# Where a head pair's k and v parts and the gates live: from three SBUF pools to the latents' pool and DRAM

## The chip, the cores and the metric

The kernel runs on one core of one Trainium2 chip. The metric is the time of one execution in device microseconds, from three runs. Engines are named as in the profile: PE is TensorE (PEld its weight loads), DVE VectorE, ACT ScalarE, POOL GpSimd, SP SyncE, which here issues nearly all DMAs.

## The reference

Two layers work on 512 tokens of width 2048. The first is a pooling mixer with a SiLU gate. The second, which this change touches, is latent attention with 16 heads, block-causal in blocks of 128 queries:

```python
c = rmsnorm(c, kv_latent_g)
kv = (c @ kv_w_b).reshape(B, S, N_HEADS, QK_NOPE + V_HEAD)
q = (rmsnorm(q_lat, q_latent_g) @ w_q_b).reshape(B, S, N_HEADS, QK_HEAD)
o = chunk_causal_attention(q, k, v).reshape(B, S, W_B)
return x + (o * jax.nn.silu(gate)) @ w_out
```

The gate is a product of the normalised stream with 2048 columns of `w_in`; each head has 128 of them. k and q get a norm over 192 elements and a rotary part of 64.

## The kernel before

Every float32 matrix product is done as three products of float32r parts: an operand is split into hi (a cast on ACT) and lo (a subtraction on DVE), and hi·hi, hi·lo and lo·hi are added in PSUM. `split` and `load_w` do this, so each weight tile of 128x512 costs a DMA issue on SP, a cast on ACT (L125) and a subtraction on DVE (L126). Raw weight tiles have three buffers, the parts four.

The kernel is written with a tile framework: the program says what is computed, and pools give out buffers under a tag. A scheduler places the instructions on each engine in its own order when the program is built and gives each tile a free buffer of its pool. The pools that matter here are `apool` (32 tiles of 128x512, called the latents' pool here), `bpool` (32), `xpool` (16) and the temporary pool `tpool3` (7).

After the first layer the stream is spilled to DRAM (L485) and two normalised copies stand as parts in `apool` and `bpool`. From them come the k/v latent and the q latent: four pairs of parts each, 16 tiles of `apool`, which every head pair reads. Then come the gates: `gate_unit` (L576 on) multiplies a head's gate columns, scales the result into a temporary tile, and writes the SiLU of it to a tile of `apool`, which is kept to the end. Sixteen gates and the two latents fill `apool`. The parts of the stream for the gates stay in `bpool` until the last gate.

Heads go in eight pairs. The preparation of a pair (`prep_units`) loads the weights, makes four k/v products, one for each block of 128 tokens (`kv_unit`, L612 to L614), and from each a raw k and the parts of v, then k statistics, four q products (L632 to L634) with their rotary part on POOL (L680 to L683), q statistics, and six transposes (`tr_unit`, L708 and L695) whose results are split. Raw k stands in two tiles of `xpool`; v in four tiles of `bpool`, or of `xpool` for the first pair.

The attention of a pair (`attn_units`) has, for each head, four score units (L738; the maximum L741, its scaling L743, Exp L746, all for one block of queries, with up to 512 keys), then four transposes of P (L757), and two P·V units (L782 to L784). The second P·V unit ends with the product of output and gate (L787), in place of the gate.

The order of the program is written at the end of the file. Attention units of pair n and preparation units of pair n+1 are merged by due times: `LEAD` (0.421 of a pair) says how far preparation goes ahead, `PACE` stretches the attention. For the last pair the units merged in are others: `og_unit`, which splits the gated output of a head, and `out_unit`, the output product for three of the 16 column blocks, head by head (L143 to L145 there). Gate units 0 to 11 stand before the preparation of pair 0, gate units 12 to 15 after it. At the end come the other column blocks, each added to the spilled stream (`out_store`).

Of the kernel before, what the change touches and what calls it, by code (L numbers as in the profile page):

```python
# [7 lines left out]
F32 = mybir.dt.float32  # L8
F32R = mybir.dt.float32r
I32 = mybir.dt.int32  # L10
AF = mybir.ActivationFunctionType
# [3 lines left out]
P = 128  # L15
S = 512
# [5 lines left out]
NH = 16  # L22
# [29 lines left out]
def trunk_kernel(  # L52
# [16 lines left out]
    nc = tc.nc  # L69
    V, A, G, T = nc.vector, nc.scalar, nc.gpsimd, nc.tensor  # L70
# [4 lines left out]
    dpool = ctx.enter_context(tc.tile_pool(name="dpool", bufs=16, space=bass.MemoryType.DRAM))  # L75

    def xt(shape=(P, S), dt=F32):
        return xpool.tile(list(shape), dt, tag="x", name="xt")

    def at(dt=F32R):  # L80
        return apool.tile([P, S], dt, tag="a", name="at")

    def bt(shape=(P, S), dt=F32R):
        return bpool.tile(list(shape), dt, tag="b", name="bt")
# [4 lines left out]
    def tt_(n=S, dt=F32):  # L89
        return tp[0].tile([P, n], dt, tag="t", name="tt_")  # L90
# [4 lines left out]
    def sc():  # L95
        return ps.tile([P, S], F32, tag="sc", name="sc", bufs=2)
# [4 lines left out]
    def f(ap):  # L101
        return ap.bitcast(F32)
# [13 lines left out]
    def load_w(src, n, parts=None):  # L116

        raw = wpool.tile([P, S], F32, tag="raw", name="raw")
        if parts is None:
            hi = wpool.tile([P, S], F32R, tag="whi", name="whi", bufs=4)  # L120
            lo = wpool.tile([P, S], F32R, tag="wlo", name="wlo", bufs=4)
        else:
            hi, lo = parts(), parts()
        nc.sync.dma_start(raw[:, :n], src)
        A.copy(hi[:, :n], raw[:, :n])  # L125
        V.tensor_tensor(lo[:, :n], raw[:, :n], f(hi[:, :n]), ALU.subtract)  # L126
        return hi, lo

    def proj(w, nk, xs, m=P, acc=None):

        acc = acc or mm()
        c = S // m if m == P else 4
        for k0 in range(0, nk, c):
            hi, lo = load_w(w[:, k0 * m:(k0 + c) * m], c * m)
            for j in range(c):
                k = k0 + j
                mm3(acc[:m, :], hi[:, j * m:(j + 1) * m], lo[:, j * m:(j + 1) * m], xs[k],
                    k == 0, k == nk - 1)
        return acc
# [7 lines left out]
    def split(src, hi, lo):  # L147
        A.copy(hi, src)
        V.tensor_tensor(lo, src, f(hi), ALU.subtract)
# [112 lines left out]
    with ExitStack() as c1:  # L262
# [91 lines left out]
        with ExitStack() as c2:  # L354
            hp = c2.enter_context(tc.tile_pool(name="hp", bufs=2, **tile_))
            for j in range(NJ):
# [5 lines left out]
                hi = w7.tile([P, 4, 2, P], F32R, tag="hi", name="hi")  # L362
                lo = w7.tile([P, 4, 2, P], F32R, tag="lo", name="lo")
# [8 lines left out]
                a, b = xh[j], xl[j]  # L372
# [46 lines left out]
    apool = ctx.enter_context(tc.tile_pool(name="apool", bufs=32, **tile_))  # L419
# [8 lines left out]
    def pooled_tile(g, o):  # L428
        x = tt_()
        nc.sync.dma_start(x, raws[g * 8 + o])  # L430
        if g:
            x = pool_tile(x, g * 8 + o in neg, WINS[g])
        hi, lo = at(), at()
        split(x, hi, lo)
        return hi, lo
# [15 lines left out]
    for g in range(NG):  # L451
        ys = [y_tile(g, o, pooled) for o in range(8)]
        if g == 0:
            rope_tables()
            for k in range(KD):
                x = xt()
# [14 lines left out]
    for k in range(KD):  # L471
        hi, lo = at(), at()
        gsplit(xr[k], C_GKV + k, hi, lo)
        xkv.append((hi, lo))
        hi, lo = bt(), bt()
        gsplit(xr[k], C_GB + k, hi, lo)
        xb.append((hi, lo))
        if k < 2:
            A.activation(accs[k], xr[k], AF.Square)
        else:  # L480
            sq = tt_()
            A.activation(sq, xr[k], AF.Square)
            V.tensor_tensor(accs[k % 2], accs[k % 2], sq, ALU.add)
        dsp = dpool.tile([P, S], F32, tag="dsp", name="dsp")
        nc.sync.dma_start(dsp, xr[k])  # L485
        spill.append(dsp)
# [10 lines left out]
    def latent_norm(lat, gcol):  # L497
        ac = tt_()
        A.activation(ac, lat[0], AF.Square)
        for o in range(1, 4):  # L500
            sq = tt_()
            A.activation(sq, lat[o], AF.Square)
            V.tensor_tensor(ac, ac, sq, ALU.add)
        r = norm_r(ac, 512)
        res = []
        for o in range(4):
            V.scalar_tensor_tensor(lat[o], lat[o], cs[:, gcol + o:gcol + o + 1], r, ALU.mult, ALU.mult)
            hi, lo = at(), at()
            split(lat[o], hi, lo)
            res.append((hi, lo))  # L510
        return res
# [62 lines left out]
    gates = []  # L574

    def gate_unit(o):  # L576
        acc = proj(bwin[4 + o], KD, xb)
        z = tt_()
        V.tensor_tensor(z, acc, rb[0], ALU.mult)
        sg = at(F32)  # L580
        A.activation(sg, z, AF.Silu)
        gates.append(sg)


    gqk = const.tile([P, 1], F32, name="gqk")
    V.tensor_tensor(gqk, cs[:, C_GKN:C_GKN + 1], cs[:, C_GQN:C_GQN + 1], ALU.mult)
    SC = 192.0 ** -0.5
    st = {}

    def small(n=8, tag="sm", bufs=6):  # L590
        return spool.tile([P, n], F32, tag=tag, name=tag, bufs=bufs)

    def hg_begin(hg):
        d = {}
        d["kvw"] = [load_w(wkvb[hg, :, k * 512:(k + 1) * 512], 512) for k in range(4)]
        d["kraw"] = [xt((P, 2, 256)) for _ in range(2)]
        d["qraw"] = [None] * 4
        vt = bt if hg else xt
        d["vh"] = [vt((P, 2, 256), F32R) for _ in range(2)]
        d["vl"] = [vt((P, 2, 256), F32R) for _ in range(2)]  # L600
        d["ssk"] = small(8, "ssk", 2)
        d["ssq"] = small(8, "ssq", 2)
        st[hg] = d
# [122 lines left out]
    def score_unit(hg, h, i):  # L726
        d = st[hg]
        n = (i + 1) * P
        s = sc()
        kh, kl = d[("T", h)]  # L730
        krh, krl = d["kr"][h]
        qh, ql_ = d[("T", 3 + h)]
        qr = d["qr"][h]
        qs = slice(i * P, (i + 1) * P)
        ops = [(qh[:, qs], kh[:, 0:n]), (qh[:, qs], kl[:, 0:n]), (ql_[:, qs], kh[:, 0:n]),
               (qr[:, qs], krh[:, 0:n]), (qr[:, qs], krl[:, 0:n])]
        for j, (l, r) in enumerate(ops):
            T.matmul(s[:, 0:n], l, r, start=(j == 0), stop=(j == 4))  # L738
        V.memset(s[0:64, n - 64:n], -1e30)
        nm = small(1, "nm", 4)  # L740
        V.tensor_reduce(nm, s[:, 0:n], AX.X, ALU.max)  # L741
        rq = d["rq"][:, 2 * i + h:2 * i + h + 1]
        V.scalar_tensor_tensor(nm, nm, -1.0, rq, ALU.mult, ALU.mult)  # L743
        pe = tt_()
        sm = small(1, "sm", 4)
        A.activation(pe[:, 0:n], s[:, 0:n], AF.Exp, bias=nm, scale=rq, accum_out=sm)  # L746
        V.reciprocal(sm, sm)
        V.tensor_scalar(pe[:, 0:n], pe[:, 0:n], sm, None, ALU.mult)
        d[("P", h, i)] = pe
# [18 lines left out]
    def pv_unit(hg, h, pr):  # L768
        d = st[hg]
        if pr == 0:  # L770
            d["ov"] = ps.tile([P, S], F32, tag="ov", name="ov", bufs=1)
        ov = d["ov"]
        js = range(2 * pr + 2)
        for j in js:
            c0 = P if j == 2 * pr + 1 else 0
            dst = ov[:, pr * 256 + c0:pr * 256 + 256]
            ph = d["pth"][j // 2][:, j % 2, c0:256]
            pl = d["ptl"][j // 2][:, j % 2, c0:256]
            vh = d["vh"][j // 2][:, j % 2, h * P:(h + 1) * P]
            vl = d["vl"][j // 2][:, j % 2, h * P:(h + 1) * P]  # L780
            last = j == js[-1]
            T.matmul(dst, vh, ph, start=(j == 0), stop=False)  # L782
            T.matmul(dst, vh, pl, start=False, stop=False)
            T.matmul(dst, vl, ph, start=False, stop=last)  # L784
        if pr == 1:
            gt = gates[2 * hg + h]
            V.tensor_tensor(gt, ov, gt, ALU.mult)  # L787

    def prep_units(hg):
        def q(t):  # L790
            q_unit(hg, t)
            qrot_unit(hg, t)

        f = {"B": lambda: hg_begin(hg), "K": lambda: kstats_unit(hg), "S": lambda: qstats_unit(hg)}
        for t in range(4):
            f[f"k{t}"] = lambda t=t: kv_unit(hg, t)
            f[f"q{t}"] = lambda t=t: q(t)
        for u in range(6):
            f[f"T{u}"] = lambda u=u: tr_unit(hg, u)
        return [f[o] for o in PREP]  # L800
# [16 lines left out]
    ogs = [None] * NH  # L817

    def og_unit(h):
        nt = at if h < 14 else bt  # L820
        hi, lo = nt(), nt()
        split(gates[h], hi, lo)
        ogs[h] = (hi, lo)

    first3 = {}
# [13 lines left out]
        V.tensor_tensor(x, x, acc, ALU.add)  # L839
        nc.sync.dma_start(outT[o], x)  # L840

    nhg = NH // 2
    for o in range(12):
        gate_unit(o)
    for u in prep_units(0):
        u()
    for o in range(12, NH):
        gate_unit(o)
# [23 lines left out]
    for u in fill[j:]:  # L872
        u()
    og_unit(14)
    og_unit(15)
    for o in range(NO, NO + 2):
        for k0, n in ((0, 4), (4, 4), (8, 4), (12, 2)):
# [69 lines left out]
```

## Time and profile before

| | |
|---|---|
| three runs, median (lowest, highest) | 1953.45 us (1952.83, 1954.7) |
| the profiled execution | 1959.55 us, span 1957.8 us |
| mean granted TensorE clock | 0.997 |
| PE, PEld, DVE, ACT, POOL busy | 1924.6, 1712.1, 1274.9, 819.9, 257.9 us |
| instructions | 30554 |
| DMA, mean | 120 GB/s |

Busy times are sums of instructions on an engine over one profiled execution. Matmuls are pipelined, so PE's busy time says that a matmul was under way, not that PE was at its peak. Stages by time: the spill starts near 1120 us; spill, latents and gates follow until near 1497, attention until 1811, and the output product until the end.

### The profile page before, as it was taken

Reading aid. Unit: us, or ns where it says so; the run is one execution under the profiler, and the core shown is the slowest. Engines: PE = TensorE matmul, PEld = TensorE weight load, DVE = VectorE, ACT = ScalarE, POOL = GpSimd, SP = SyncE. Lnnn points to the kernel's source line nnn. Section 1 sums busy time; section 2 is a strip of 40 time slices with the busy share of each in tenths; the row PEclk is TensorE's granted clock in tenths of the full one; section 3 lists DMA queues with packets and bytes.
Section 4 is the critical chain, followed back from the end, with each engine's and each line's share of the span. In section 5 each row is a group of like instructions: output and inputs, shape, how many; then the busy total and the mean of one; then the engine's idle time right before and its main releaser. Section 6 shows DMA issues by size and latency. Waiting matters only on the chain.

```text
span 1957.8 us, 30554 instructions
## 1 busy us (share of the span) xinstructions
PE 1924.6 (98%) x11356; PEld 1712.1 (87%) x11356; DVE 1274.9 (65%) x2289; ACT 819.9 (42%) x1562; POOL 257.9 (13%) x405
## 2 busy tenths in 40 slices
PE   7999999999999999999999999999999999999999
PEld 6999999999999878888888888888888888888887
DVE  8577786796666677486595567473344788797432
ACT  7343333333333443233333354333254777785221
POOL 0433332333233100000000000000010111110000
PEclk9999999999999999999999999999999999999999
DMA  6454444435443464344344344323322111121632
GB/s 190 149 160 154 150 132 127 130 119 164 134 135 125 151 209 158 109 124 144 119 128 130 111 148 128 92 92 99 97 93 79 53 42 47 50 68 49 219 118 86
DMA packets 167893, 235.52 MB, mean 120 GB/s; under 512 B 14656, under 2 KB 94912, under 8 KB 167744
## 3 DMA queue, kind: packets, MB, share of 16 engines
q1 hardware_dynamic: 166992, 232.84, 37.8%
q8 instruction: 89, 1.46, 0.3%
q10 hardware_dynamic: 720, 0.73, 0.1%
q14 instruction: 60, 0.49, 0.1%
q0 software_dynamic: 32, 0.00, 0.0%
HBM read 208.35 MB, written 25.17 MB: 119 GB/s over the span
## 4 chain that ended last, share of the span: by engine, by line
PE 89%; DVE 4%; DMA 3%; ACT 2%; issue 1%; SPq 0%; DVEq 0%; ACTq 0%
PE mm L145 16%; PE mm L143 16%; PE mm L144 16%; PE k L331 9%; PE k L329 9%; PE k L327 9%; PE sc L738 2%; PE mm L612 2%; DMA raw<-awin 2%; PE mm L614 2%; PE mm L613 2%; DVE lo L311 1%; PE k L378 1%; PE mm L632 1%; PE k L379 1%
## 5 line engine op out<-in xcount | busy, mean ns | idle before, releaser
L125 ACT CAST whi<-raw 128x512 fp32r<-128x512 f32 (+2 forms) x421 | 253.4, 609 | 519.8 <-PE mm L144 448.0
L329 PE MATMUL k<-xl,hi 128*128 128x256 f32 x1680 | 460.7, 283 | 0.0
L327 PE MATMUL k<-xh,hi 128*128 128x256 f32 x1680 | 460.7, 283 | 0.0
L126 DVE TENSOR_TENSOR wlo<-raw,whi 128x512 fp32r<-128x512 f32 (+2 forms) x421 | 281.4, 671 | 235.2 <-ACT whi L125 233.2
L331 PE MATMUL k<-xh,lo 128*128 128x256 f32 x1680 | 418.8, 284 | 2.6 <-DVE lo L311 2.5
L310 ACT CAST hi<-raw 128x1792 fp32r<-128x1792 f32 x120 | 202.8, 1690 | 368.2 <-PE k L331 248.2
L311 DVE TENSOR_TENSOR lo<-raw,hi 128x1792 fp32r<-128x1792 f32 x120 | 248.1, 2068 | 158.3 <-ACT hi L310 158.0
L145 PE MATMUL mm<-bt,wlo 128*128 128x512 f32 x860 | 335.5, 390 | 0.2 <-DVE wlo L126 0.2
L143 PE MATMUL mm<-bt,whi 128*128 128x512 f32 x860 | 334.6, 389 | 0.0
L144 PE MATMUL mm<-bt,whi 128*128 128x512 f32 x860 | 334.5, 389 | 0.0
L327 PEld LDWEIGHTS k<-xh,hi 128*128 128x128 f32 x1680 | 323.3, 192 | 0.0
L329 PEld LDWEIGHTS k<-xl,hi 128*128 128x128 f32 x1680 | 323.2, 192 | 0.0
L331 PEld LDWEIGHTS k<-xh,lo 128*128 128x128 f32 x1680 | 297.5, 192 | 4.2 <-DVE lo L311 3.6
L143 PE MATMUL mm<-at,whi 128*128 128x512 f32 x516 | 201.9, 393 | 4.2 <-ACT whi L125 4.2
L145 PE MATMUL mm<-at,wlo 128*128 128x512 f32 x516 | 202.7, 393 | 0.6 <-DVE wlo L126 0.3
L144 PE MATMUL mm<-at,whi 128*128 128x512 f32 x516 | 202.7, 393 | 0.0
L145 PEld LDWEIGHTS mm<-bt,wlo 128*128 128x128 f32 x860 | 161.4, 188 | 34.5 <-DVE wlo L126 0.6
L143 PEld LDWEIGHTS mm<-bt,whi 128*128 128x128 f32 x860 | 161.5, 188 | 33.8 <-ACT whi L125 0.2
L144 PEld LDWEIGHTS mm<-bt,whi 128*128 128x128 f32 x860 | 161.5, 188 | 33.4
L306 POOL TENSOR_TENSOR raw<-raw 128x256 f32<-128x256 f32 x120 | 99.4, 828 | 440.6 <-DVE raw L304 415.8
L143 PEld LDWEIGHTS mm<-at,whi 128*128 128x128 f32 x516 | 97.4, 189 | 25.1 <-ACT whi L125 5.3
L145 PEld LDWEIGHTS mm<-at,wlo 128*128 128x128 f32 x516 | 97.6, 189 | 22.7 <-DVE wlo L126 2.6
(1151 smaller groups left out, 2584.0 us busy)
## 6 DMA issues: line engine op xcount, KB each, us to landing
raw<-awin SPq DMA_DIRECT2D x240, 256.0 KB, 3.2
raw<-awo SPq DMA_DIRECT2D x128, 256.0 KB, 2.9
raw<-bwin SPq DMA_DIRECT2D x80, 256.0 KB, 2.7
raw<-awg SPq DMA_DIRECT2D x64, 256.0 KB, 2.8
raw<-bwo SPq DMA_DIRECT2D x59, 256.0 KB, 2.8
scr<-e SPq DMA_DIRECT2D x56, 256.0 KB, 2.7
raw<-wkvb SPq DMA_DIRECT2D x32, 256.0 KB, 2.9
raw<-wqb SPq DMA_DIRECT2D x32, 192.0 KB, 2.4
```

The source lines that it names most:

```text
L125: A.copy(hi[:, :n], raw[:, :n])
L126: V.tensor_tensor(lo[:, :n], raw[:, :n], f(hi[:, :n]), ALU.subtract)
L143: T.matmul(dst, wh, xh, start=first, stop=False)
L144: T.matmul(dst, wh, xl, start=False, stop=False)
L145: T.matmul(dst, wl, xh, start=False, stop=last)
L306: G.tensor_tensor(c[:, :, 6, :], c[:, :, 4, :], c[:, :, 2, :], ALU.add)
L310: A.copy(hi, c[:, :, 1:8, :])
L311: V.tensor_tensor(lo, c[:, :, 1:8, :], f(hi), ALU.subtract)
L327: T.matmul(dst, hi[:, j % 2, wi, :], xh[j][:, xi, :], start=first, stop=False, skip_group_check=True)
L329: T.matmul(dst, hi[:, j % 2, wi, :], xl[j][:, xi, :], start=False, stop=False, skip_group_check=True)
L331: T.matmul(dst, lo[:, j % 2, wi, :], xh[j][:, xi, :], start=False, stop=last, skip_group_check=True)
L612: T.matmul(acc, ch[:, tsl], hi, start=(k == 0), stop=False)
```

## The change

k products and v parts of every pair are taken from `apool`, which has 16 buffers for this once the gates are out of it. A gate unit writes SiLU in place in its temporary tile and stores it to DRAM. At the third score unit of a head its gate is loaded to a tile of `apool`. The product with the output is made there; for the first seven pairs the result is stored to DRAM, over the gate, and for the last pair the tile is kept. `og_unit` loads the gated output of heads 0 to 13 into a temporary tile and splits it from there; heads 0 to 7 have their parts in `apool`, the others in `bpool` (before: 0 to 13 and 14 to 15).

```diff
-    def at(dt=F32R):
-        return apool.tile([P, S], dt, tag="a", name="at")
+    def at(dt=F32R, shape=(P, S)):
+        return apool.tile(list(shape), dt, tag="a", name="at")
@@ gate_unit
-        sg = at(F32)
-        A.activation(sg, z, AF.Silu)
-        gates.append(sg)
+        A.activation(z, z, AF.Silu)
+        gd = dpool.tile([P, S], F32, tag="gd", name="gd")
+        nc.sync.dma_start(gd, z)
+        gates.append(gd)
@@
-    st = {}
+    st, gated = {}, {}
+    nhg = NH // 2
@@ hg_begin
-        d["kraw"] = [xt((P, 2, 256)) for _ in range(2)]
+        d["kraw"] = [at(F32, (P, 2, 256)) for _ in range(2)]
         d["qraw"] = [None] * 4
-        vt = bt if hg else xt
-        d["vh"] = [vt((P, 2, 256), F32R) for _ in range(2)]
-        d["vl"] = [vt((P, 2, 256), F32R) for _ in range(2)]
+        d["vh"] = [at(F32R, (P, 2, 256)) for _ in range(2)]
+        d["vl"] = [at(F32R, (P, 2, 256)) for _ in range(2)]
@@ score_unit
+        if i == 2:
+            gt = d[("G", h)] = at(F32)
+            nc.sync.dma_start(gt, gates[2 * hg + h])
@@ pv_unit
         if pr == 1:
-            gt = gates[2 * hg + h]
+            gt = d.pop(("G", h))
             V.tensor_tensor(gt, ov, gt, ALU.mult)
+            if hg == nhg - 1:
+                gated[2 * hg + h] = gt
+            else:
+                nc.sync.dma_start(gates[2 * hg + h], gt)
@@ og_unit
-        nt = at if h < 14 else bt
+        nt = at if h < 8 else bt
         hi, lo = nt(), nt()
-        split(gates[h], hi, lo)
+        if h < 14:
+            x = tt_()
+            nc.sync.dma_start(x, gates[h])
+        else:
+            x = gated[h]
+        split(x, hi, lo)
```

## Rows read from the trace of the kernel before

**Rows 1.** Page, busy time of each engine, its share and instructions.
```profile
PE 1924.6 (98%) x11356; PEld 1712.1 (87%) x11356; DVE 1274.9 (65%) x2289; ACT 819.9 (42%) x1562; POOL 257.9 (13%) x405
```
**Rows 2.** Busy time by stage: stretch, its length, PE, PEld, DVE, ACT, POOL, clock, DMA.
```profile
1213.00:1400.00 187.00, 187.00 (x823) 152.79 (x822) 95.30 (x166) 57.43 (x103) 0.00 (x0) 1.00 0.30 94
1400.00:1500.00 100.00, 99.49 (x463) 83.61 (x462) 41.34 (x91) 40.98 (x103) 6.13 (x16) 1.00 0.30 93
1500.00:1560.00 60.00, 56.61 (x325) 50.15 (x324) 42.63 (x155) 44.09 (x152) 8.89 (x24) 1.00 0.16 48
1597.00:1635.00 38.00, 37.00 (x222) 32.64 (x220) 31.18 (x112) 28.40 (x97) 6.02 (x16) 1.00 0.17 50
...
1711.00:1749.00 38.00, 37.01 (x220) 32.50 (x218) 33.57 (x107) 29.44 (x95) 5.96 (x15) 1.00 0.16 50
1749.00:1768.00 19.00, 17.01 (x92) 14.06 (x91) 18.07 (x63) 15.70 (x48) 4.57 (x10) 1.00 0.28 89
1768.00:1811.00 43.00, 42.97 (x249) 37.37 (x248) 29.57 (x89) 21.39 (x56) 0.00 (x0) 1.00 0.17 50
```
**Rows 3.** PE's waits from 1597 to 1811 us: total us, times, longest.
```profile
PE ov L783 <- DVE xt L149: 1.0, 4, 0.3
PE mm L612 <- DVE bt L149: 0.6, 4, 0.2
...
PE sc L738 <- ACT tt__18145 L746: 1.4, 1, 1.4
```
**Rows 4.** Instructions in order of time, DVE, POOL, ACT: start, us, engine, line.
```profile
1621.63 0.15 DVE L743 SCALAR_TENSOR_TENSOR nm<-nm,qy 128x1 f32<-128x1 f32 x1
...
1631.47 0.47 POOL L680 TENSOR_TENSOR tt__16400<-xt,qcos 128x128 f32<-128x128 f32 x1 [25.07 <-ACT xt L637]
1631.89 0.32 POOL L681 TENSOR_TENSOR tt__16401<-xt,qsin 128x64 f32<-128x64 f32 x1
...
1633.03 0.45 ACT L746 ACTIVATE tt__16429<-sc,nm,qy 128x128 f32<-128x128 f32 x1
```
**Rows 5.** DMA issues: count, KB each, median us from issue to landing.
```profile
raw<-bwo SPq DMA_DIRECT2D x59, 256.0 KB, 2.8
...
dsp<-xt SPq DMA_DIRECT2D x16, 256.0 KB, 2.1
```
**Rows 6.** SP's own waits from 1560 to 1749 us: total us, times, longest.
```profile
SPq L124 <- DVE wlo L126: 148.5, 12, 20.0
```
**Rows 7.** ACT's waits from 1500 to 1810 us.
```profile
ACT whi L125 <- DMA raw<-wkvb: 1.4, 3, 1.0
```
**Rows 8.** Groups of instructions from 1735 to 1760 us: busy us, mean ns, idle before.
```profile
L149 DVE TENSOR_TENSOR at<-at 128x512 fp32r<-128x512 f32 x12 | 8.1, 680 | 0.0
L148 ACT CAST at<-at 128x512 fp32r<-128x512 f32 x12 | 7.5, 639 | 0.8 <-DVE at L149 0.8
```
**Rows 9.** Readers of the latents' pool, 1480 to 1830 us: ns, first and last start.
```profile
L143 PE MATMUL mm<-at,whi x42: 389/390/498, 1748.6 to 1799.0; 128*128 128x512 f32 x42
```
**Rows 10.** ACT in order of time: two scores' Exp of pair 6, head 1.
```profile
1763.96 0.60 ACT L746 ACTIVATE tt__18373<-sc,nm,qy 128x256 f32<-128x256 f32 x1
...
1770.94 0.67 ACT L746 ACTIVATE tt__18441<-sc,nm,qy 128x384 f32<-128x384 f32 x1 [1.72 <-DVE nm L743]
```
**Rows 11.** Busy time of lines 143, 144, 145 from 1749 to 1768 us: PE, PEld.
```profile
1749.00:1768.00 19.00, 6.07 (x16) 2.81 (x15) 1.00 0.28 89
...
1749.00:1768.00 19.00, 6.10 (x16) 2.83 (x15) 1.00 0.28 89
...
1749.00:1768.00 19.00, 5.59 (x14) 2.63 (x14) 1.00 0.28 89
```
**Rows 12.** Chain of waits in order of time: start, us, two scores of a pair.
```profile
1597.14 2.02 PE sc L738 x10
1635.16 2.02 PE sc L738 x10
...
1711.23 2.02 PE sc L738 x10
...
1753.77 2.29 PE sc L738 x10
```

More of the change, by code (lines that the diff above doesn't have):

```diff
@@ L840, in out_store @@
         nc.sync.dma_start(outT[o], x)
-    nhg = NH // 2
     for o in range(12):
```

## The prediction

> **What bounds the kernel now.** I read the page's engine line first, then busy time by stage, PE's waits, the chain of waits, and last the rows of single instructions where the pools decide an order. PE is busy 1924.6 of 1957.8 us [rows 1]: 33.2 us of idle time is all that a change without a matmul more or less can give back, and only what lies behind the gates is in reach of this one. By stage [rows 2]: from 1213 to 1400 us (the latents, then the gates) PE has no idle time; 0.51 us from 1400 to 1500; 3.39 us where attention starts (1500 to 1560); then periods of 38.0 us, one a head pair, with 1.00 us idle each (two of five alike are shown: 5.0 us); 1.99 us from 1749 to 1768 and 0.03 us after that, to 1811. Together 10.9 us. The waits name the causes [rows 3]: a score's PSUM bank that waits for Exp, a P·V product that waits for the split of P, a k/v product that waits for the split of v. No long wait stands there, and DVE with 31.2 of 38 us is loaded, not full.
>
> What orders the work is less plain. The tile numbers grow in program order, and in the rows a pool's slots are first written in the order in which the program first writes them. The first score of a pair has its maximum scaled at 1621.63; its Exp runs at 1633.03, right after GpSimd has begun on the q rotation's tiles (tt__16400 at 1631.47, tt__16401 at 1631.89), which the program writes before it in the same pool [rows 4]. It stood 11.3 us for its turn. So every pool is a queue, and moving tiles from one pool to another changes who waits for whom.
>
> **The change, part by part.** The sum is made against the profiled execution: 1959.55 us, of which 1957.8 are its span; the median of the three timed runs, 1953.45, is 6.1 us below it, and I take the difference over to the median.
>
> (a) Gates stored. Silu writes in place instead of into the latents' pool: the same 16 ACT and 16 DVE instructions. New are 16 stores of 256 KB, each standing in SP's queue until Silu is done, with weight loads behind it. 823 matmuls in 187 us are 0.227 us each [rows 2], so a gate (48) takes 10.9 us, and a store adds 262 KB in that time, 24 GB/s beside 94. A 256 KB store lands in 2.1 us, a load in 2.8 [rows 5]. The cover is the three raw weight tiles, 12 matmuls or 2.7 us each, 8.2 us; a load that leaves late by the two instructions between the last matmul and the store (DVE and ACT, 0.68 and 0.64 us on a 128x512 tile [rows 8]) and lands in 2.8 us stays inside. Cost 0. Without the cover each store could cost a landing, 16 x 2.8 = 45 us; the nearest row, no idle time in the stage, says 0, and I keep 0 to +3.
>
> (b) Gates loaded at the third score, gated tiles stored: 16 loads and 14 stores, 0.33 us of SP each. In the steady periods SP sat 148.5 of 189 us waiting for a raw tile [rows 6], so it has room; 7.9 MB over 310 us is 25 GB/s beside some 50. A gate is wanted only at the end of its head, behind its fourth score and all its P·V products. In the latents' pool 16 of 32 slots are left beside the two latents: v of three pairs 12, k products 2, two gates: 16, and for a moment 18, when the third token block of the next k/v product wants its three tiles before the transposes have freed the previous k products. That block then waits, as it does today for its turn in another pool. Cost 0; bounds 0 to +4 (0.25 us on each of 16 heads, as large as the largest steady wait).
>
> (c) k products and v leave the queues of the two other pools. Today a k/v product can be emptied only when the pairs of P tiles that the program writes earlier in that pool have been written. Afterwards it queues behind two gate loads alone, so kv, and with it q, the rotation and the Exp of [rows 4], can come some us sooner. This gives back only idle time of PE: at most the 5.0 us of the steady periods and what the start has over them, 3.39 - 1.58 = 1.8 us, together -6.8. It could also lose: the order is new, and a second gap of the size of the old one in each period would be +5.0. The nearest direct row is the 0.6 us in four waits for the split of v [rows 3]; I take -1.5 for the periods and -1.0 for the start, together -2.5.
>
> (d) The reload at the end. Today the 12 head splits that the last pair's out products need run between 1735 and 1760 (8.1 us of DVE, 7.5 of ACT [rows 8]), as soon as the latents free their slots, and PE's first out product starts at 1748.6 [rows 9]. Afterwards each split waits for a load into the temporary pool, which has seven slots, and in that pool's order. The first reload stands behind the Exp of the second score of pair 6, head 1 (1763.96), the next three behind the third (1770.94) [rows 10], the fourth score behind these. So in the 19 us from 1749 to 1768 PE loses its filler: 16 + 16 + 14 out matmuls [rows 11] x 0.227 = 10.4 us of 17.0 busy. If the chain of scores kept its times, 12.4 us would be idle, 10.4 more than now: the upper bound. But that chain was pushed back by those very splits: scores that start 38.02 us apart (1597.14, 1635.16; then 1711.23) come 42.5 us after the last, 4.5 us late, at 1753.77 [rows 12]. Without 15.6 us of splits on ACT and DVE it should keep its pace, and the first reload be split at about 1764 (1763.96 - 4.5 for that Exp, 2.8 us of landing, 1.3 us of split). I take 4 us idle where there were 2.0: +2.0, bounds -2 (no idle time left) and +10.4. Out products that are put off cost nothing later, since from 1768 on PE has no idle time: they only move behind it.
>
> Sum: 0 + 0 - 2.5 + 2.0 = -0.5; 1959.05 for a profiled execution like this one, 1953.0 for the median.
>
> **The rivals.** *The gaps close (faster).* The small waits all go and the tail keeps its pace: -5.0 in the periods, -1.8 at the start, +1.8 for the tail: 1948.5. For it: the gaps repeat from period to period, and the 11.3 us of [rows 4] shorten. Against: the rows name Exp, a split and PSUM banks, which the change does not touch. Here a rule of the Trainium skill bears, Trace Analysis, section Optimization Strategy: the same gap repeating on the engine that should be saturated can mean that SBUF is too small for the next tile. By that rule all 10.9 us go, 1942.6; the trace agrees that the gap repeats, but the releasers are instructions and not slots.
>
> *The end starves (slower).* The reloads come in single file: seven slots hold the rotation's two tiles, up to five score tiles that by the program's order wait for their transposes, and so hardly more than one reload, of some 5 us (landing, split, turn). PE then idles 10 us between 1749 and 1785 instead of 2: +8, less 1.5 from (c): 1960. It decides from the point where the first out product starts after 1770. For it: the order in the pool [rows 4]. Against: the delayed scores [rows 12].
>
> *SP's queue (slower).* A store waits for the product of gate and output, and weight loads behind it come late, where a split already waits for its load at times (1.4 us in three waits, the longest 1.0 [rows 7]). 0.6 us in each of 16 heads, +9.6: 1963. Against: SP's long idle waits [rows 6]. That a gate comes too late, because its slot is not free, and so the change does not do what it says, ends in the same place: DVE waits, and the scores behind it.
>
> **How the numbers follow.** Forecast 1953.0 with chance 0.42 (own range 1949.6 to 1957.3); gaps close 0.30; the end starves 0.22; SP's queue 0.06. About 0.2% (3.9 us) is what a measurement of this kernel tells from no change. Faster 0.30, within 0.42, slower 0.28. The range goes from 1946.5 (all of (c), nothing lost) to 1961 (the end starves, a little more than its price).
>
> **What would show it.** (a) No idle time of PE while the gates run. (b) Gates landing several us before the product that reads them; no wait of a weight split for a DMA. (c) First scores' Exp earlier against the q transposes; PE's idle time per period under 1.0 us. (d) The first out product at 1760 to 1768, head splits no longer in 1735 to 1760, and 3 to 5 us idle there. I am wrong if a period grows longer than 38.0 us, if PE waits for a DMA, or if the tail is idle over 8 us.

## The result and the profile after

The changed kernel takes 1958.62 us (median of 18 runs, 1956.41 to 1961.66), the kernel before 1954.72 us (18 runs, 1952.83 to 1957.86): a ratio of 1.002, 95% interval 1.0013 to 1.0027. It is 3.9 us slower. The prediction was 1953.0, no change; the wide range held the time, the forecast's own range (to 1957.3) did not.

The profiled execution of after took 1959.75 us, its span is 1958.0: level with the execution profiled before. That is an accident of the execution before. Its last gate product came 3.8 us later than after's (1496.0 against 1492.2 us), behind code that is the same in both but for the gate stores; part of it is one more stretch at 1.2 GHz in the first layer (mean granted clock from 460 to 720 us 0.98, in after 0.99). So the two traces are compared from the first score on, which starts at 1505.3 us before and 1501.4 after: the same place of the program stands 3.9 us earlier in after's trace. The page's engine line, and busy time by stage (columns as in [rows 2]):

```profile
PE 1924.0 (98%) x11356; PEld 1712.6 (87%) x11356; DVE 1274.9 (65%) x2289; ACT 817.6 (42%) x1562; POOL 255.2 (13%) x405
```
```profile
1213.00:1400.00 187.00, 187.00 (x824) 153.21 (x823) 93.60 (x164) 57.77 (x104) 0.00 (x0) 1.00 0.35 107
1400.00:1500.00 100.00, 99.44 (x463) 83.56 (x462) 41.43 (x93) 41.53 (x107) 6.13 (x16) 1.00 0.37 112
1500.00:1560.00 60.00, 57.02 (x332) 50.51 (x331) 45.87 (x167) 45.27 (x154) 8.80 (x24) 1.00 0.25 75
1597.00:1635.00 38.00, 36.63 (x221) 32.45 (x220) 31.01 (x111) 27.83 (x97) 5.72 (x16) 1.00 0.25 76
...
1749.00:1768.00 19.00, 16.48 (x88) 14.35 (x87) 16.03 (x56) 14.19 (x40) 3.11 (x8) 0.82 0.45 137
```
```profile
1745.10:1764.10 19.00, 16.31 (x89) 14.23 (x88) 16.23 (x58) 12.73 (x39) 3.11 (x8) 0.82 0.40 125
```

Against [rows 2]: the stage of the gates is unchanged. A stretch of 38 us has 1.37 us idle instead of 1.00. And 1749 to 1768 has a mean granted clock of 0.82 where it was 1.00; the last line is the same place of the program, 3.9 us earlier, with 2.69 us idle where there were 1.99.

Three stretches with ends of each kernel's own add up: first score to last q product, from there to the last P·V product, and from there to the last matmul. The kernel before, then after (same columns):

```profile
1505.30:1748.10 242.80, 234.45 (x1389) 207.12 (x1388) 197.31 (x697) 182.08 (x609) 37.91 (x101) 1.00 0.16 51
1748.10:1818.90 70.80, 68.78 (x388) 58.99 (x387) 51.59 (x161) 40.89 (x113) 5.47 (x12) 1.00 0.26 79
1818.90:1953.50 134.60, 134.60 (x597) 111.45 (x595) 42.93 (x66) 30.00 (x50) 0.00 (x0) 1.00 0.44 139
```
```profile
1501.40:1743.90 242.50, 232.63 (x1381) 205.94 (x1380) 194.39 (x700) 177.95 (x610) 36.61 (x103) 1.00 0.24 74
1743.90:1819.40 75.50, 72.75 (x397) 62.75 (x395) 54.93 (x158) 42.83 (x112) 3.86 (x10) 0.95 0.48 152
1819.40:1953.80 134.40, 134.40 (x596) 111.27 (x594) 42.93 (x66) 29.98 (x50) 0.00 (x0) 1.00 0.42 135
```

From the first score to the last matmul: 448.2 before, 452.4 after, +4.2 us, about the difference of the medians. PE's idle time is length less busy time: 8.35 and 2.02 us before, 9.87 and 2.75 after, so +1.5 ahead of the last q product and +0.7 behind it. The rest is busy time: 437.83 against 439.78 us, +1.95 for the same matmuls. Half clock stands in that stretch, and the matmuls in it are longer, so most of this is the clock. The size is rough: the versions below that keep 2.4 GHz with the same matmuls lie between 437.76 (e8) and 438.83 us (e2). The stretch behind the last q product is 4.7 us longer, but 1.8 us of that is work that stood ahead of the last q product before.

Where the clock falls is seen in finer stretches; before, then after:

```profile
1746.00:1750.00 4.00, 3.90 (x23) 3.38 (x22) 3.29 (x8) 4.00 (x15) 3.88 (x8) 1.00 0.00 0
1750.00:1753.00 3.00, 2.36 (x13) 1.73 (x11) 3.00 (x11) 3.00 (x10) 0.54 (x1) 1.00 0.28 87
1753.00:1760.00 7.00, 6.23 (x35) 5.42 (x36) 6.73 (x20) 5.96 (x16) 0.00 (x0) 1.00 0.44 140
```
```profile
1746.00:1750.00 4.00, 3.16 (x21) 2.41 (x19) 3.98 (x12) 2.32 (x6) 0.00 (x0) 1.00 0.41 134
1750.00:1753.00 3.00, 1.67 (x11) 1.20 (x11) 2.72 (x9) 3.00 (x11) 1.29 (x4) 0.98 0.76 251
1753.00:1760.00 7.00, 6.48 (x26) 6.23 (x27) 5.41 (x26) 4.24 (x15) 1.82 (x5) 0.52 0.25 80
```

After's PE is idle for 2.17 of the 7 us from 1746 to 1753 (0.74 before), and then its granted clock is at half, 1.2 GHz, for 6.83 us. What stands there, from PE's instructions in order of time (in brackets the idle time ahead of one and what ended it):

```profile
1748.73 0.66 PE L697 MATMUL tr<-cs,tt__18098 128*128 128x128 f32 x4 [0.23 <-DVE xt L149]
1750.83 0.55 PE L744 MATMUL sc<-bt 128*128 128x128 f32 x3 [1.44 <-ACT tt__18261 L752]
1752.03 0.66 PE L710 MATMUL tr<-cs,at 128*128 128x128 f32 x4 [0.18 <-DVE bt L149]
1753.52 1.01 PE L744 MATMUL sc<-bt 128*128 128x256 f32 x3 [0.83 <-ACT tt__18300 L752]
...
1760.90 0.94 PE L143 MATMUL mm<-at,whi 128*128 128x512 f32 x3
```

Two scores wait for a PSUM bank that Exp is still reading, 1.44 and 0.83 us; before it was two as well, 1.41 [rows 3] and 0.48 us. But the first out product comes at 1760.90, 17 us behind the last q product; before it came 0.5 us behind it [rows 9], and 24 out matmuls stood ahead of the two score waits and between them. Why so late: the first and the second reload on SP, and the split of the first on ACT. It was issued at 1751.92, took 3.4 us to land, and then stood some 4 us for its turn on ACT:

```profile
1751.92 0.33 SPq L834 DMA_DIRECT2D tt__18484<-gd  x1
...
1759.41 0.32 SPq L834 DMA_DIRECT2D tt__18507<-gd  x1
```
```profile
1759.64 0.62 ACT L148 CAST at<-tt__18484 128x512 fp32r<-128x512 f32 x1
```

PE's waits from 1597 us to the last q product of after (1744), against [rows 3]; and SP's waits in the periods, against [rows 6]:

```profile
PE ov L788 <- DVE nm L749: 2.4, 4, 0.6
PE tr L710 <- DVE xt L149: 1.1, 4, 0.3
PE ov L788 <- ACT xt L148: 0.7, 4, 0.2
```
```profile
SPq L124 <- DVE wlo L126: 62.8, 17, 13.3
SPq L797 <- DVE xt L149: 45.0, 5, 9.0
```

The waits of a k/v product for the split of v and of a P·V product for DVE's split of P are gone, and three others took their place: 0.6, 0.3 and 0.2 us in every pair.

### The profile page after: what moved, and what is told of

The parts are those of the page before. It is cut to its first block, busy times and chain, and to the rows that moved or that the text cites. A ratio compares the mean times of both kernels' runs of the same rounds, so it can differ in the third digit from the quotient of the medians.

```text
span 1958.0 us, 30656 instructions
## 1 busy us (share of the span) xinstructions
PE 1924.0 (98%) x11356; PEld 1712.6 (87%) x11356; DVE 1274.9 (65%) x2289; ACT 817.6 (42%) x1562; POOL 255.2 (13%) x405
## 4 chain that ended last, share of the span: by engine, by line
PE 89%; DVE 3%; DMA 3%; ACT 3%; issue 1%; SPq 0%; ACTq 0%; DVEq 0%
PE mm L145 16%; PE mm L143 16%; PE mm L144 16%; PE k L331 9%; PE k L329 9%; PE k L327 9%; PE sc L744 2%; DMA raw<-awin 2%; PE mm L614 2%; PE mm L615 1%; PE mm L616 1%; DVE lo L311 1%; PE k L378 1%; PE k L379 1%; PE k L380 1%
## 5 line engine op out<-in xcount | busy, mean ns | idle before, releaser
L145 PE MATMUL mm<-bt,wlo 128*128 128x512 f32 x944 | 368.3, 391 | 0.2 <-DVE wlo L126 0.2
L143 PE MATMUL mm<-bt,whi 128*128 128x512 f32 x944 | 367.4, 390 | 0.0
L144 PE MATMUL mm<-bt,whi 128*128 128x512 f32 x944 | 367.2, 389 | 0.0
L145 PEld LDWEIGHTS mm<-bt,wlo 128*128 128x128 f32 x944 | 177.3, 188 | 38.2 <-DVE wlo L126 1.1
L143 PEld LDWEIGHTS mm<-bt,whi 128*128 128x128 f32 x944 | 177.2, 188 | 36.7 <-ACT whi L125 0.2
L144 PEld LDWEIGHTS mm<-bt,whi 128*128 128x128 f32 x944 | 177.3, 188 | 36.6
L143 PE MATMUL mm<-at,whi 128*128 128x512 f32 x432 | 167.9, 392 | 3.3 <-ACT whi L125 3.3
L145 PE MATMUL mm<-at,wlo 128*128 128x512 f32 x432 | 169.2, 392 | 0.5 <-DVE wlo L126 0.5
L144 PE MATMUL mm<-at,whi 128*128 128x512 f32 x432 | 169.3, 392 | 0.0
L306 POOL TENSOR_TENSOR raw<-raw 128x256 f32<-128x256 f32 x120 | 102.9, 857 | 438.4 <-DVE raw L304 421.2
L307 POOL TENSOR_TENSOR raw<-raw 128x256 f32<-128x256 f32 x120 | 101.8, 849 | 9.2
L143 PEld LDWEIGHTS mm<-at,whi 128*128 128x128 f32 x432 | 81.2, 189 | 20.8 <-ACT whi L125 4.4
```

Source lines behind the costliest of these rows:

```text
L143: T.matmul(dst, wh, xh, start=first, stop=False)
L144: T.matmul(dst, wh, xl, start=False, stop=False)
L145: T.matmul(dst, wl, xh, start=False, stop=last)
L306: G.tensor_tensor(c[:, :, 6, :], c[:, :, 4, :], c[:, :, 2, :], ALU.add)
L307: G.tensor_tensor(c[:, :, 7, :], c[:, :, 6, :], c[:, :, 3, :], ALU.add)
```

## Theories and experiments

**A, the tail.** The reload makes the out products late; PE is idle a few times in succession among the last pairs' scores, and its granted clock falls. **B, traffic.** The 60 new DMAs of 256 KB (16 gate stores, 16 gate loads, 14 stores and 14 reloads of gated outputs) load the DMA engines and SP's queue. **C, the new place of k and v.** It makes the periods longer.

Each experiment ran beside the kernel before on the same chip, and its ratio is to those runs. The clock is the mean granted clock of a kernel's runs (the kernel before: 0.9987 to 0.9989 in the groups of the experiments). Idle time is PE's in the profiled execution, from the first score to the last q product and from there to the last P·V; then the half clock within these, and the length from first score to last matmul.

| kernel | median us | ratio to before (95%) | clock | idle us | half clock us | length us |
|---|---|---|---|---|---|---|
| before | 1954.7 to 1955.5 | | 0.9987 to 0.9989 | 8.4 + 2.0 | 0 | 448.2 |
| after | 1958.62 | 1.0020 (1.0013 to 1.0027) | 0.9965 | 9.9 + 2.7 | 6.83 | 452.4 |
| e1 reload by another pool | 1961.60 | 1.0036 (1.0022 to 1.0050) | 0.9970 | 10.0 + 3.9 | 6.83 | 454.4 |
| e2 gates by DRAM alone | 1957.23 | 1.0010 (1.0002 to 1.0019) | 0.9988 | 9.1 + 1.9 | 0 | 449.8 |
| e3 k and v back | 1957.68 | 1.0019 (1.0010 to 1.0027) | 0.9972 | 8.3 + 2.9 | 6.83 | 451.3 |
| e4 reload alone | 1957.71 | 1.0016 (1.0008 to 1.0025) | 0.9979 | 8.3 + 2.9 | 3.41 | 450.5 |
| e5 first four early | 1963.81 | 1.0044 (1.0031 to 1.0058) | 0.9968 | 11.9 + 3.9 | 6.83 | 457.1 |
| e6 after, P·V thrice | 1957.28 | 1.0008 (0.9999 to 1.0016) | 0.9983 | 9.6 + 0.7 | 3.41 | 451.2 |
| e7 copy, no DMA | 1958.83 | 1.0015 (1.0007 to 1.0024) | 0.9977 | 8.4 + 3.1 | 6.83 | 452.2 |
| e8 last heads kept | 1957.03 | 1.0012 (1.0003 to 1.0020) | 0.9981 | 10.1 + 1.8 | 0 | 449.6 |
| e9 kept, k and v back | 1955.66 | 1.0001 (0.9993 to 1.0010) | 0.9991 | 8.6 + 1.6 | 0 | 448.7 |
| e10 before, P·V thrice | 1954.50 | 0.9998 (0.9989 to 1.0007) | 0.9993 | 8.3 + 0.1 | 0 | 448.2 |
| e11 e9, P·V thrice | 1959.99 | 1.0024 (1.0014 to 1.0034) | 0.9983 | 8.4 + 2.6 | 0 | 452.0 |
| e12 e8, P·V thrice | 1959.63 | 1.0024 (1.0015 to 1.0033) | 0.9978 | 10.4 + 1.7 | 3.41 | 452.6 |

The clock of a run is given to 0.001, which is 2 us of the time, so a mean over ten runs is good to some 0.5 us by estimate.

### Which part holds the loss: e1 to e4

**e1**, after with the reload through the second pool:

```diff
-            x = tt_()
+            x = bt(dt=F32)
             nc.sync.dma_start(x, gates[h])
```

> The changed kernel with one edit: a gated output comes back through a tile of the second pool (32 buffers), not of the temporary pool (7). Theory A (the tail: the reloads stand behind the scores in the temporary pool, so PE has no out product between 1749 and 1760 us, is idle there a few times in succession, and its granted clock falls to half for 6.8 us): first out product within 6 us of the last q product, granted clock 1.00 from 1740 to 1770, 4 us or more off the changed kernel, about 1954.5 or a ratio to the kernel before of 0.999 to 1.001. Theory B (traffic: 46 more DMAs in SP's queue and on the DMA engines): nothing changes, 1958 to 1959. Theory C (k and v parts in the latents' pool make each period longer): nothing changes, 1958 to 1959.

None of the three theories said this: 3 us slower than after (five runs). The loads left earlier, five in a row, but ACT's split of the first stands 16 us behind its issue (SP, then ACT, in order of time):

```profile
1749.23 2.33 SPq L834 DMA_DIRECT2D bt<-gd  x5
```
```profile
1765.07 0.62 ACT L148 CAST at<-bt 128x512 fp32r<-128x512 f32 x1
```

So the narrow temporary pool is not what alone makes the reload late; in this build the loads have left and the split still comes late on ACT. Why it stands there was not settled.

**e2**, the gates stored and loaded, the gated tile kept, no reload; k and v in their old pools:

```diff
-            if hg == nhg - 1:
-                gated[2 * hg + h] = gt
-            else:
-                nc.sync.dma_start(gates[2 * hg + h], gt)
+            gated[2 * hg + h] = gt
@@ og_unit
-        nt = at if h < 8 else bt
+        nt = at if h < 14 else bt
-        if h < 14:
-            x = tt_()
-            nc.sync.dma_start(x, gates[h])
-        else:
-            x = gated[h]
-        split(x, hi, lo)
+        split(gated[h], hi, lo)
@@ hg_begin: k products and v in xt and bt, as before
```

> Gates through DRAM alone: stored after the gate stage and loaded at a head's third score as in the changed kernel, but the gated tile is kept in the latents' pool to the end, and k products and v parts are back in the two pools of the kernel before; no reload at the end. Theory A: as the kernel before, ratio 0.9995 to 1.0005, first out product at its place of before, granted clock 1.00 in the tail. Theory B: 32 of the 60 new transfers are here, so about half of the loss, +2 us (ratio 1.001) or more. Theory C: as the kernel before.

No half clock, tail as before, as A says; but 2 us slower, as B says. Its profile has two score waits (1.2 and 1.1 us, behind other pairs) that neither before nor after has, and PE waits for no DMA in it, so the build's order is the likelier cause. But the profile fell on its fastest execution (1954.36 us), so where its median loses 2.4 us stays open. It is not a price that every kernel with these transfers pays: e3 and e4 (next) differ only in that e3 also takes the gates through DRAM (32 transfers), and their medians are the same.

**e3**, after with k and v back in the old pools, and **e4**, the kernel before with the store and reload of gated outputs alone:

```diff
 e3, hg_begin
-        d["kraw"] = [at(F32, (P, 2, 256)) for _ in range(2)]
+        d["kraw"] = [xt((P, 2, 256)) for _ in range(2)]
+        vt = bt if hg else xt
-        d["vh"] = [at(F32R, (P, 2, 256)) for _ in range(2)]
+        d["vh"] = [vt((P, 2, 256), F32R) for _ in range(2)]
 e4, pv_unit
             V.tensor_tensor(gt, ov, gt, ALU.mult)
+            if hg < NH // 2 - 1:
+                gd = dpool.tile([P, S], F32, tag="gd", name="gd")
+                nc.sync.dma_start(gd, gt)
+                gates[2 * hg + h] = gd
@@ og_unit
-        nt = at if h < 14 else bt
+        nt = at if h < 8 else bt
-        split(gates[h], hi, lo)
+        x = gates[h]
+        if h < 14:
+            x = tt_()
+            nc.sync.dma_start(x, gates[h])
+        split(x, hi, lo)
```

> The changed kernel with k products and v parts back in the two pools of the kernel before; gates and gated outputs through DRAM with the reload at the end stay. Theory A: as the changed kernel or within 1 us of it, ratio to the kernel before 1.0015 to 1.0025, with a late first out product and some us of half clock in the tail. Theory C: the loss goes, ratio 0.9995 to 1.0005, periods back at 38.02 us. Theory B: as the changed kernel, but with the idle time as waits for DMAs or for weight parts and not in the tail.

> The kernel before with the end of the change alone: gates stay in the latents' pool, k and v in their old pools, but the gated outputs of the first seven pairs are stored to DRAM and come back through the temporary pool, head by head, at the end. Theory A: the whole loss is here, +3.5 to +5 us (ratio 1.0018 to 1.0026), with the first out product 10 us or more later than in the kernel before and half clock in the tail. Theory B: 28 of 60 new transfers, at most half of the loss, +1 to +2 us. Theory C: as the kernel before.

Both come out as A in kind: the reload alone costs 2.9 us in the median, a little under the 3.5 that A named, with the first out product 14 us behind the last q product and half clock in the tail. With k and v in their old pools the idle time ahead of the last q product is back at 8.3 us.

### The mechanism of the tail: e5, e6, e7, e10

**e7**, the kernel before without any new DMA; GpSimd copies the gated output into the temporary pool where after loads it. **e6**, after with 24 needless matmuls right ahead of the idle gaps:

```diff
 e7, og_unit
-        split(gates[h], hi, lo)
+        x = gates[h]
+        if h < 14:
+            x = tt_()
+            G.tensor_copy(x, gates[h])
+        split(x, hi, lo)
 e6, pv_unit
-        for j in js:
+        again = 3 if (hg, h, pr) == (nhg - 3, 1, 1) else 1
+        for j in [j for _ in range(again) for j in js]:
```

> The kernel before, no new DMA and gates kept on chip, but the gated output of heads 0 to 13 is copied by GpSimd into a tile of the temporary pool (7 tiles, shared with the scores) ahead of its split, in the place where the changed kernel loads it. Theory A (the queue in the temporary pool, not the transfers): first out product 10 us or more later than in the kernel before, half clock in the tail, +3 to +5 us, ratio 1.0015 to 1.0026. Theory B (transfers, SP's queue): as the kernel before, ratio 0.9995 to 1.0005.

> The changed kernel with 24 needless matmuls: the second P V unit of pair 5, head 1, which stands right ahead of the idle gaps, computes its sum three times over (the first two are overwritten). That is 24 x 0.115 = 2.8 us more for PE. Theory A: PE is not idle there, the granted clock stays at 1.00 in the tail (no 6.8 us at 1.2 GHz, 3.4 us saved) and the idle 2.5 us is mostly taken: 1 to 4 us faster than the changed kernel in spite of the added work, 1955 to 1957.5. If the clock has nothing to do with the idle gaps: 0 to 2.8 us slower than the changed kernel, with half clock still there.

e7 first, then e6 (stretches with the same columns as above):

```profile
1746.00:1750.00 4.00, 2.81 (x20) 2.18 (x18) 4.00 (x12) 2.73 (x7) 0.00 (x0) 1.00 0.43 137
1750.00:1753.00 3.00, 1.38 (x9) 1.17 (x9) 2.65 (x9) 3.00 (x11) 1.86 (x6) 0.62 0.46 162
1753.00:1760.00 7.00, 7.00 (x36) 6.57 (x35) 5.85 (x27) 4.40 (x16) 2.33 (x5) 0.67 0.02 6
```
```profile
1746.00:1750.00 4.00, 4.00 (x38) 4.00 (x37) 3.61 (x12) 2.91 (x7) 0.00 (x0) 1.00 0.58 192
1750.00:1753.00 3.00, 2.51 (x18) 1.79 (x17) 2.98 (x11) 3.00 (x13) 2.23 (x7) 1.00 0.52 173
1753.00:1760.00 7.00, 6.77 (x42) 5.68 (x42) 6.91 (x32) 4.60 (x13) 0.58 (x2) 1.00 0.43 128
```

e7 has no transfer more than the kernel before and loses 3.3 us, with 3.1 us idle in the tail (after 2.7) and the same 6.83 us at 1.2 GHz: for the tail, B falls. What PE waits for there is not the same in every build: in after it is two scores, in e7 two transposes that wait for DVE's splits (1.2 and 1.6 us), and so in e3 and e4. Common to them is that no out product stands there. e6 does more work than after and is 1.3 us faster (by the ratios 2.3 us; the intervals overlap a little), its tail at full clock. What is lost there is PE's idle time and the clock that goes with it. e6 shows one thing more: it has half clock in a period, and what comes right before it is the new wait that the place of k and v brings (0.6 us ahead of a P·V product). The same wait stands in every pair of after, and its clock stays at 2.4 GHz there:

```profile
1620.00:1622.00 2.00, 1.26 (x10) 0.89 (x9) 1.94 (x7) 0.64 (x2) 0.00 (x0) 1.00 0.00 0
1622.00:1626.00 4.00, 4.00 (x20) 3.78 (x21) 1.88 (x7) 2.45 (x10) 1.42 (x5) 0.57 0.41 131
```

**e10**, the control: the same edit on the kernel before, with `NH // 2` for `nhg`.

> The kernel before with the same 24 needless matmuls as in the earlier run on the changed kernel (second P V unit of pair 5, head 1, three times over). Here the tail has its out products and keeps its clock, so theory A says that the added 2.8 us are paid but for the part of the 2.0 us idle there that they fill: 0.8 to 2.8 us slower than the kernel before, ratio 1.0004 to 1.0015. If needless matmuls help in themselves, this kernel gets faster too.

Not slower, a small miss. Behind the last q product 0.06 us are idle instead of 2.02, and PE's busy time from the first score on is 439.81 us, 2.0 more than before: the 24 matmuls cost about 2.0 us, not 2.8, and just fill the idle time. So a needless matmul is free where PE is idle, and worth something only where it keeps the clock.

**e5**, the repair that failed: heads 0 to 3 loaded and split ahead of the last pair's preparation.

```diff
+            if hg == nhg - 2:
+                due += [hg - LEAD] * 4
+                fill += [lambda h=h: og_unit(h) for h in range(4)]
@@ fill of the last pair: og_unit from head 4 on
@@ og_unit
-        nt = at if h < 8 else bt
+        nt = at if 4 <= h < 12 else bt
-            x = tt_()
+            x = at(F32) if h < 4 else tt_()
```

> The changed kernel, but the gated outputs of heads 0 to 3 are loaded and split before the last pair's preparation (load to a tile of the latents' pool, parts in eight tiles of the second pool, which the change left free), so 36 out matmuls wait ready when the last q product is done. Theory A (idle PE in the tail, then half clock): granted clock 1.00 from 1740 to 1770, first out product within 4 us of the last q product, about 4.5 us off the changed kernel: 1953 to 1955, ratio to the kernel before 0.999 to 1.000, and the mean granted clock of the runs back at 0.999. Theory B (60 more DMAs) and theory C (k and v parts in the latents' pool): 1958 to 1959, ratio 1.002, since all DMAs and the place of k and v stay.

The first out product came 2.7 us behind the last q product, as wanted, but that product itself came 5 us later than in after, measured from the first score, with idle time and half clock ahead of it (the stretch before 1749):

```profile
1711.00:1749.00 38.00, 34.47 (x199) 30.05 (x198) 29.25 (x101) 26.10 (x87) 4.33 (x12) 0.96 0.28 91
```

The early parts take eight tiles of the pool that the last pair's preparation needs; that this delays it is argued, not shown.

### A tail that has work without a reload: e8, e9, e11, e12

**e8**, after, but the gated outputs of pairs 5 and 6 stay on chip, and the out products begin with heads 10 and 11. **e9**, e8 with k and v in their old pools.

```diff
-            if hg == nhg - 1:
+            if hg >= nhg - 3:
                 gated[2 * hg + h] = gt
@@ og_unit
-        nt = at if h < 8 else bt
-        if h < 14:
+        nt = at if h < 6 or h in (10, 11) else bt
+        if h < 10:
@@ out_unit: the first head of a sum is 10 in place of 0, in two lines
@@ fill of the last pair, and the units after it
-            for k0, n in ((0, 4), (4, 4), (8, 4), (12, 2)):
+            for k0, n in ((10, 2), (0, 4), (4, 4), (8, 2), (12, 2)):
```

> The changed kernel, but the gated outputs of pairs 5 and 6 stay on chip like those of pair 7 (the latents' pool has room once the k/v latent is out), and the output products begin with heads 10 and 11 instead of 0; ten reloads are left. So 18 out matmuls (4.1 us) need no load. Theory A (idle PE among the scores of the tail, then half clock): first out product within 3 us of the last q product, granted clock 1.00 from 1740 to 1770, 3 to 5 us off the changed kernel: 1953.5 to 1956, ratio to the kernel before 0.9990 to 1.0005, full-clock span unchanged or 1 us less. Theory B (transfers): 8 of 60 fewer, 1958. Theory C (place of k and v): 1958 to 1959.

> As the run before it (last heads kept, products from head 10 on), with k products and v parts back in the two pools of the kernel before. Theory A: the same time as that run within 1.5 us, 1953.5 to 1956.5, granted clock 1.00 in the tail. Theory C: 1 us or more faster than that run, since the periods go back from 38.22 to 38.02 us (5 x 0.2 us).

In both profiles the tail keeps 2.4 GHz. e9 is level with the kernel before; e8 took back 1.6 of 3.9 us, less than A said, and is 1.4 us slower than e9, which C said and A allowed. The stretches to the last q product and to the last P·V, and PE's waits from 1597 to 1745 us, of e8 and then of e9:

```profile
1502.00:1744.60 242.60, 232.55 (x1381) 205.90 (x1381) 194.97 (x701) 178.54 (x611) 36.57 (x103) 1.00 0.24 72
1744.60:1817.20 72.60, 70.81 (x397) 60.35 (x395) 53.49 (x161) 42.23 (x115) 3.90 (x10) 1.00 0.47 145
```
```profile
PE ov L788 <- DVE nm L749: 2.4, 4, 0.6
PE tr L710 <- DVE xt L149: 1.3, 4, 0.5
PE ov L788 <- ACT xt L148: 0.6, 4, 0.2
```
```profile
1500.60:1744.30 243.70, 235.15 (x1392) 207.44 (x1391) 197.31 (x704) 181.62 (x612) 38.27 (x103) 1.00 0.19 61
1744.30:1814.20 69.90, 68.31 (x383) 58.12 (x381) 52.66 (x158) 42.12 (x113) 4.89 (x11) 1.00 0.44 133
```
```profile
PE ov L790 <- DVE xt L149: 1.0, 4, 0.2
PE mm L615 <- DVE bt L149: 0.5, 3, 0.2
```

The waits go with the place of k and v, whatever the tail does: 10.1 us idle against 8.6. The mean clock is 0.9981 against 0.9991, 2 us, though neither profile has half clock from the first score on.

**e11** and **e12** put the needless matmuls of e6 into e9 and e8 (the same edit), as a try for a kernel faster than both.

> The run with the last heads kept on chip and k and v parts back in their old pools (1955.7 us), with the 24 needless P V matmuls of before added. If idle PE in the tail is all that is left to gain, 1954 to 1956, level with the kernel before (ratio 0.9990 to 1.0005), granted clock 1.00 in the tail and at 0.999 in the mean of the runs.

> The same with k and v parts in the latents' pool, as the change has them. Theory A alone (the tail is all): the same time as the run beside it, within 0.7 us. Theory C in a new form (k and v parts in the latents' pool leave a 0.6 us gap in each period, after which the granted clock sometimes falls to half for 3.4 us): 1 to 2 us slower than the run beside it, all of it in the mean granted clock of the runs (0.998 against 0.999), and where the profile shows half clock in attention it begins just after such a gap.

e11 missed its range by 4 us. The build's order changed with the edit, and in both a score in the tail now waits 1.6 us for Exp (e12, then e11):

```profile
1763.33 0.74 PE L744 MATMUL sc<-bt 128*128 128x128 f32 x3 [1.60 <-ACT tt__18523 L752]
```
```profile
1762.66 0.55 PE L745 MATMUL sc<-bt 128*128 128x128 f32 x3 [1.60 <-ACT tt__18523 L753]
```

The clock falls to 1.2 GHz for 3.41 us behind this one gap in e12, and stays at 2.4 GHz behind the same gap in e11. The two medians differ by 0.4 us, as A said (within 0.7) and the other way round from C, though e12 again has 2.0 us more idle time ahead of the last q product and the lower clock. So that the place of k and v brings idle time stands in all three pairs (after and e3, e8 and e9, e12 and e11: 1.5 to 2.0 us); that this costs time is not shown: medians +0.9, +1.4, -0.4 us, and by the ratios +0.2, +2.2, 0. What it does show is that the gain forecast for it did not come. No version beat the kernel before.

## Why the prediction was wrong

(a) Gate stores, 0: right. No idle time from 1213 to 1400 us; 0.56 us instead of 0.51 from 1400 to 1500.

(b) Gate loads and gated stores, 0: right for the loads, PE waits for no DMA. SP does wait for gated outputs with weight loads behind them (45.0 us in five waits), and PE waits for no weight part in a period for it. One sign named for this part did not hold, at no cost to PE that a row shows: ACT waited for loads of out weights, at 1749 and at 1800 us (ACT's waits from 1500 to 1810 us, against [rows 7]):

```profile
ACT whi L125 <- DMA raw<-bwo: 3.6, 2, 2.3
```

(c) k and v out of the other queues, -2.5: the sign failed. The queue did shorten: the first Exp of a pair, which stood 11.3 us for its turn [rows 4], stands 3.6 us (maximum scaled on DVE, rotation on POOL, Exp on ACT, three answers):

```profile
1624.61 0.14 DVE L749 SCALAR_TENSOR_TENSOR nm<-nm,qy 128x1 f32<-128x1 f32 x1
```
```profile
1627.17 0.46 POOL L682 TENSOR_TENSOR tt__16433<-xt,qcos 128x128 f32<-128x128 f32 x1 [24.04 <-ACT xt L639]
```
```profile
1628.32 0.48 ACT L752 ACTIVATE tt__16463<-sc,nm,qy 128x128 f32<-128x128 f32 x1
```

The step that failed is "This gives back only idle time of PE", with -1.5 for the periods chosen "by the nearest row", the 0.6 us of waits for the split of v. Those waits went, and the waits of P·V products and transposes for DVE and ACT took their place: the loss that the step itself allowed for (up to +5.0 for a second gap in each period) and did not take. In after's trace the start gave back 0.4 us of idle time (2.98 instead of 3.39 in its first 60 us) and the periods lost 1.9: +1.5 instead of -2.5, 4.0 us of the 4.7 between the sum and the trace. In the medians the gain is missing too: after is 0.9 us slower than e3, which has k and v in their old pools. The first sign named for being wrong came true: the first q products of two pairs now stand 38.2 us apart (1575.0 and 1613.2), not 38.0.

The rule weighed there, from the Trainium skill (Perfetto Trace Analysis, section Optimization Strategy; a repeating gap can mean too little SBUF for the next tile), did not decide here: the slots came and the gaps stayed, 1.37 us a period instead of 1.00.

(d) The reload, +2.0: right in direction and place. The first out product came at 1760.90, inside the foreseen 1760 to 1768; counted from the first score the first split, at 1759.64, stands at 1763.5 of the trace before, where about 1764 was foreseen. Idle time in these 19 us is 2.69 us (2.52 by the clock time of [rows 2]) instead of 1.99, less than the 4 us taken: the chain of scores did come earlier, as argued from [rows 12] (the score at 1753.77 there starts at 1745.10 in after, 4.8 us earlier from the first score; forecast 4.5). What the sum lacked is the clock, a second failed step. "Out products that are put off cost nothing later" holds for the products, but without them the idle time lies close together, and 6.83 us at 1.2 GHz follow, some 1.95 us of PE time in this execution. With 0.7 us of idle time that makes 2.7; the parts alone measured 2.9 (e4) and 3.3 us (e7). Over many runs the clock's share may be larger: (1 - 0.9965) x 1957 = 6.8 us against 2.1 to 2.6 for the kernel before, an upper bound, since a half-clock stretch also covers waits that would have been idle.

The rivals: the gaps did not close. The end starved, and 1960 was near, but its deciding point (first out product after 1770) was not reached, and its price, 10 us of idle time, was not paid: a right time by a wrong mechanism. SP's queue is out for the tail by e7.

The Trainium skill has a rule that bears on the term left out: TensorE: Matmul & The Clock Gate, section "A second HAM failure mode: psum-queue depth-cycling", says that short idle times between groups of matmuls, when frequent, can make the clock go back and forth between its levels. The traces agree in part: no idle gap of after's tail is longer than 1.44 us, and the clock falls 0.2 us into the fourth of a row (0.23, 1.44, 0.18, 0.83 us). But in e12 one gap of 1.60 us stands alone ahead of the fall, and the same gap in e11 left the clock as it was, so which gaps it takes is not shown here.

## What to carry to other kernels

Where PE is 97% busy, price a lost filler twice: by the idle time that it leaves, and by the clock that may fall behind short gaps (in these runs of 0.6 to 1.6 us, and not each time); give the tail work that needs nothing late (e9 did so by starting with heads still on chip). Freeing one queue can move a wait to the next resource, as here, unless the row says that this queue is what PE waits for. And compare mean granted clocks over many runs: one profile shows one of several outcomes.

## What was not expected of the hardware

The granted clock of an engine that is 98% busy fell to 1.2 GHz behind gaps of 0.23, 1.44 and 0.18 us and early in a fourth, of 0.83 us, all between 1748 and 1754 us, and came back after 6.83 us; in before, gaps of 1.41 and 0.48 us with 12 out matmuls between left it at 2.4 GHz. The same gap can do both: 1.60 us in e12 (half clock) and in e11 (none), 0.6 us in a period of e6 (half clock) and in those of after (none). Half clock does not double the time there: 6.83 us at 1.2 GHz added 1.95 us of busy time (after), 2.3 (e3) and 2.9 (e7), each good to about 1 us, where double time would be 3.4. And 24 more matmuls made a kernel faster by 1.3 us in the median.
